# Another order of the seven products in the MLP blocks of a two-layer decoder kernel

## The chip, the cores and the metric

The kernel runs on one core of a Trainium2 chip. The metric is the device time of one execution in microseconds (us). The engines are named as in the profile: PE multiplies matrices, ACT (ScalarE) and DVE (VectorE) read the results out of PSUM and work element by element, POOL and SP mostly issue DMAs.

## The reference

Two decoder layers over 512 tokens of width 1024, then a last norm. Each layer mixes (sliding-window attention and retention, gated) and then has an MLP; the change lies mostly in the MLP.

```python
for l in range(DEPTH):
    # h = rmsnorm(x) @ w_in; attention, retention, gates; then
    x = x + mixed @ w_out
    h2 = rmsnorm(x, g_mlp)
    x = x + jnp.square(jax.nn.relu(h2 @ w_up)) @ w_down
return rmsnorm(x, g_final)
```

## The kernel before, in words

Everything is computed in f32 precision. Each operand is kept as two parts: hi, rounded on ACT (L343 for weights, L415 for intermediate values), and lo, the rest, subtracted on DVE (L344, L416). One product of f32 operands is then three matmuls (`products`, L395 to L397: hi by hi, lo by hi, hi by lo).

The weights come in units of 128 x 1024, in one list (`unit_order`). For each unit SP loads a raw tile (a pool of five), DVE may add two raw tiles (L283 in the up part, L306 in the down part), ACT and DVE split it, and PE uses it. `unit` takes the next unit of the list and splits three ahead; `split_until` loads four ahead of the split.

The MLP of a layer is worked in eight blocks of 512 hidden columns, e = 0 to 7. In block 0 the up part is a plain product; in each later block it is two *pairs* (`pair(0)`, `pair(1)`), which multiply halves with four weight units each: pairs 6 and 7 are those of block 4. The down part (`down`) of a block multiplies 2 x 2 blocks with **seven products** instead of eight (of sums and differences of the operands), each with a unit of its own and of twelve matmuls of 512 columns:

- the first into the banks a, and ACT copies a to b (L1562);
- the second into c, read out early (L1619) with sign minus;
- the third adds into b; its left operand is a sum of hidden values, split as `r<-sums` (ACT L415, DVE L416); b is read out early;
- the fourth adds into a, the fifth into c, and both are read out for good (`put`: ACT L1619 or DVE L1609);
- the sixth adds into b, which DVE reads out (L1609, into a tile eu that already holds the early part);
- the seventh adds into b again and is read out. The sixth's readout must be over, bank by bank, before the seventh's first matmul.

What was read out is sent to a DRAM tensor y by accumulating DMAs on POOL's queue (L1624). The last block of each layer takes another way at its end (layer 1's is a plain product).

At the input of a layer the first projections go into four banks at once (`group`), and meanwhile the norm is made: token sums by four small matmuls (ssq<-ones,acc, L566), their inverse root (table load and L598 on ACT, L599 on DVE), the tile wide (L601), its split sh and sl, and two matmuls ssq<-sh and ssq<-sl (L613) that spread it over all rows. `chunk(... put_q(2))` and `put_q(3)` are the two projections behind this group.

The order on each engine is made by a scheduler when the program is built; it goes by the order of the code and by its own estimate of when things are ready, and `tc.issue_after(x)` holds what is within it behind x. On the chip each engine's queue runs strictly in that order. So the code's order of products is not quite that of PE's queue: on PE, regular blocks before have 6 matmuls of the fourth, 2 of the fifth, 4 of the third, 10 of the fifth, 8 of the third, 6 of the fourth, the sixth, twelve of the next pair, the seventh.

Of the kernel before, what the change touches and what calls it, by code (L numbers as in the profile page):

```python
# [53 lines left out]
DELAY = 2  # L54
AHEAD = 4
SPLIT = 3
CLEANED = ({1: (0,)}, {})


def unit_order(layer):  # L60

    order = [("w_in", i) for i in range(4 + 2 + 8 + 2 + 4 + 2 + 2)]
    order += [("w_a", i) for i in range(4)]
    order += [("rv", part, u) for part in range(7) for u in range(2)]
    order += [("w_in", i) for i in range(24, 34)]
    order += [("w_b", i) for i in range(4)]
    order += [("w_in", i) for i in range(34, 38)]
    order += [("w_b", i) for i in range(4, 8)]
    order += [("wo", part, u) for part in range(7) for u in range(2)]
    for e in range(N_BLOCK):  # L70
        if e == 0:
            order += [("w_up", u) for u in range(4)]
        else:
            order += [("pair", 2 * e - 2 + i, part) for i in range(2) for part in range(4)]
        if layer == DEPTH - 1 and e == N_BLOCK - 1:
            order += [("w_end", k) for k in range(4)]
        else:
            order += [("block", e, part) for part in range(7)]
    return order


# [37 lines left out]
def decoder(ctx, tc, xT, x_first, w_in, w_rv, w_a, w_b, w_wo, w_up, w_pair, w_down, w_end, tables, decay, band, g_last, out):  # L119
# [182 lines left out]
    def add_block(i):  # L302
        e, part = order[i][2:]
        if part in (2, 4) and e < N_BLOCK - 1:
            raws[i] = raws.pop(i - 2)
            nc.vector.tensor_tensor(raws[i], raws[i], raws.pop(i - 1), ALU.add)  # L306

    def load_values(i):
        layer, name, part, u = order[i]
# [133 lines left out]
    def chunk(name, layer, moving, evacuate, rate=1.0, pool=ps_mm):  # L443

        hi, lo = unit(name, layer)
        n = len(moving)
        ps = bank(pool, "mm")
        pairs = [((hi[:, k * P : (k + 1) * P], lo[:, k * P : (k + 1) * P]), moving[k]) for k in range(n)]
        advance(rate)
        products(ps, pairs[: n // 2], True, False)  # L450
        advance(rate)
        products(ps, pairs[n // 2 :], False, True)
        evacuate(ps)
# [50 lines left out]
    class Forms:  # L504
# [27 lines left out]
        def part(self, j):  # L532
            return self.f[j // 2][:, 2 * (j % 2) : 2 * (j % 2) + 2, :]
# [54 lines left out]
    class Rms:  # L588
# [20 lines left out]
        def finish(self):  # L609
            self.value = tmp.tile([P, T], F32, tag="norm", name="rstd", bufs=1)  # L610
            ps = bank(ps_aux, "ssq")
            for i, part in enumerate(self.parts):
                nc.tensor.matmul(ps, ones, part, start=i == 0, stop=i == 1)  # L613
            nc.scalar.activation(self.value, ps, AF.Copy)


# [2 lines left out]
    def layer_body(layer):  # L619
# [102 lines left out]
            else {1: carried.pop(1), 2: rms_mix.prepare, 3: stats},  # L722
            {1: carried.pop(0)} if layer else None,
        )
        chunk("w_in", layer, xs, put_q(2))
        chunk("w_in", layer, xs, put_q(3), pool=ps_aux)
        turn_v()

# [668 lines left out]
        def sum_input(ks):  # L1397

            b = big("xg")
            for i in range(2):  # L1400
                g = ks + i + 4
                col = g_mlp * KD + g
                nc.scalar.activation(b[:, i, :], x[:, g, :], AF.Copy, scale=gain[:, col : col + 1])
            first = early.pop(ks)
            sums.one(ks, first)
            sums.middle(ks, first, b, (0, 1))
            sums.rest(ks, b, (2, 3))

        def block(half, tokens):
            at = slice(tokens * H, tokens * H + H)  # L1410
# [51 lines left out]
        def pair(which):  # L1462
            def multiply(ps, weights, left, moving, start=True):
                hi, lo = weights
                cols = [slice((0 if left else 4 * P) + k * P, (0 if left else 4 * P) + (k + 1) * P) for k in range(4)]
                products(ps, [((hi[:, c], lo[:, c]), m) for c, m in zip(cols, moving)], start, True, not start)

            a, e, b = (bank(ps_mm, "mm")[:, :H] for _ in range(3))
            eu, z = temp("eu"), big("z")
            part = unit("pair", layer)
            multiply(a, part, True, block(0, 0))
            nc.scalar.activation(b, a, AF.Copy)  # L1476
            multiply(e, part, False, sums[0])
            nc.scalar.activation(eu[:, :H], e, AF.Copy)
            part = unit("pair", layer)
            multiply(b, part, True, sums[1], False)  # L1480
            nc.scalar.activation(eu[:, H:], b, AF.Copy)
            multiply(a, part, False, block(1, 0), False)
            nc.scalar.activation(z[:, 0, :H], a, AF.Relu)
            if which:
                second(z, slice(0, 1), SOON)
            part = unit("pair", layer)
            multiply(b, part, True, sums[2], False)
            nc.vector.scalar_tensor_tensor(z[:, 1, H:], b, -1.0, eu[:, :H], ALU.mult, ALU.subtract)
            multiply(e, part, False, block(1, 1), False)
            nc.vector.tensor_tensor(z[:, 0, H:], e, eu[:, H:], ALU.add)  # L1490
            nc.scalar.activation(z[:, :, H:], z[:, :, H:], AF.Relu)
            if which:
                second_late(z)
            part = unit("pair", layer)
            multiply(b, part, True, sums[3], False)
            nc.scalar.activation(z[:, 1, :H], b, AF.Relu, scale=-1.0)
            if which:
                second(z, slice(1, 2), SOON)
                second_rest(z)
            elif plain:  # L1500
                first_plain(z)
            else:
                first_two(z)
# [34 lines left out]
        def down(e, into, meanwhile=None):  # L1538
            def multiply(ps, moving, start=True):
                hi, lo = unit("block", layer)  # L1540
                for m in range(2):
                    at = slice(m * P, (m + 1) * P)
                    pairs = []
                    for k, (uh, ul) in enumerate(moving):
                        cols = slice(k * T, (k + 1) * T)
                        pairs.append(((uh[:, at], ul[:, at]), (hi[:, cols], lo[:, cols])))
                    products(ps[m], pairs, start, True, not start)

            b11 = [(first_hi[:, k, :], first_lo[:, k, :]) for k in range(2)]
            b21, b22 = (  # L1550
                [(u_two[:, k, at], u_two[:, 2 + k, at]) for k in range(2)] for at in (slice(0, H), slice(H, T))
            )
            if e == N_BLOCK - 1:
                sums.free()
            a, c = ([bank(ps_mm, "mm") for _ in range(2)] for _ in range(2))
            b = [bank(ps_aux, "b") for _ in range(2)]
            multiply(a, b11)
            with tc.issue_after(latest[0]):
                for m in CLEANED[last].get(e, ()):
                    nc.tensor.matmul(b[m], ones, xh[:, 0, :], start=True, stop=True)  # L1560
            for m in range(2):
                nc.scalar.activation(b[m], a[m], AF.Copy)  # L1562
            multiply(c, u_forms[0])
            for m in range(2):
                into.early(1, 1, m, c[m], -1)
            multiply(b, u_forms[1], False)
            for m in range(2):
                into.early(0, 1, m, b[m], 1)
            if meanwhile:
                with tc.issue_after(last_second[0]), tc.issue_after(last_second[1]):  # L1570
                    meanwhile()
            multiply(a, b21, False)
            for m in range(2):
                into.put(0, 0, m, a[m], 1)
            if e == N_BLOCK - 1:
                state["hold"] = state["next"] + 3
            multiply(c, b22, False)
            for m in range(2):
                into.put(0, 1, m, c[m], 1)
            multiply(b, u_forms[2], False)  # L1580
            for m in range(2):
                into.put(1, 1, m, b[m], -1)
            into.last_but_one()
            multiply(b, u_forms[3], False)
            if e == N_BLOCK - 1:
                into.first_weights()
            for m in range(2):
                into.put(1, 0, m, b[m], -1)
            into.end()
# [146 lines left out]
        def first_hooks():  # L1736
            used = []

            def at0():
                used.append(column_factors())  # L1740
                sum_input(0)

            def at1():
                if last:
                    used.append(bank(ps_aux, "xt"))
                    for n in range(NB):
                        turn_x(used[n % 2], n, 1)

            return at0, at1
# [196 lines left out]
```

## Time and profile before

| | us |
|---|---|
| median of three runs | 1447.37 (1445.71 to 1448.91) |
| the profiled execution | 1446.45 |
| its span (first to last instruction) | 1444.4 |
| PE busy | 1431.3 |
| DVE busy | 1166.0 |
| ACT busy | 969.6 |
| POOL busy | 222.0 |

The granted clock was 0.999 in the mean. Busy times overlap, and a matmul's end is modelled, so small stalls of PE count as busy; a stall shows in the starts of two matmuls: in a run without waits, matmuls of 512 columns start 0.23 us apart and those of 256 columns 0.11 us. In the lists of waits a row says who waited for whom, the total, how many times and the longest; in timelines a row has start, duration, engine, line, operation, the tiles written and read, and in brackets the idle time ahead of it with what ended it.

### The profile page before, as it was taken

The numbers are of one execution on the slowest core, as the hardware profiler recorded it, in microseconds if no ns is written. First come the engines' busy times: TensorE is split into PE (matmuls) and PEld (weight loads), VectorE is DVE, ScalarE is ACT, GpSimd is POOL, SyncE is SP. The second block draws the span as 40 slices with busy tenths as digits, with TensorE's granted clock in tenths as the row PEclk, the third lists the DMA queues.
The fourth block names the chain that finished last, engine by engine and source line by source line (L and its number), as shares of the span: only waits on it lengthen the run. The fifth ranks groups of instructions, "written<-read, shape, count | busy, mean of one in ns | idle before, by whom it ended". The sixth has DMA issues, their size and how long they took to land.

```text
span 1444.4 us, 22150 instructions
## 1 busy us (share of the span) xinstructions
PE 1431.3 (99%) x8041; PEld 1246.5 (86%) x8041; DVE 1166.0 (81%) x1762; ACT 969.6 (67%) x1592; POOL 222.0 (15%) x329
## 2 busy tenths in 40 slices
PE   9999999999999999999999999999999999999998
PEld 7888888888988999998888888888889799999987
DVE  6978876966998888888878789677779978888885
ACT  7657555553687777777756575565437878777775
POOL 0011012112101111112201110112120011111120
PEclk9999999999999999999999999999999999999999
DMA  7598359899745777676955983797875477777664
GB/s 267 179 288 225 103 162 305 238 245 253 234 130 197 192 201 194 176 185 182 314 172 177 290 224 105 214 299 219 227 204 185 144 203 198 195 199 195 179 188 153
DMA packets 96429, 297.57 MB, mean 206 GB/s; under 512 B 11329, under 2 KB 11457, under 8 KB 90433
## 3 DMA queue, kind: packets, MB, share of 16 engines
q0 software_dynamic: 35936, 125.58, 37.6%
q1 hardware_dynamic: 59664, 169.27, 33.6%
q8 instruction: 63, 1.03, 0.3%
q10 hardware_dynamic: 720, 1.31, 0.2%
q14 instruction: 46, 0.37, 0.1%
HBM read 256.54 MB, written 115.87 MB: 258 GB/s over the span
## 4 chain that ended last, share of the span: by engine, by line
PE 97%; ACT 2%; DVE 1%; DMA 0%; issue 0%; ACTq 0%; DVEq 0%
PE mm L395 23%; PE mm L396 23%; PE mm L397 23%; PE wo L1301 5%; PE b L395 3%; PE b L396 3%; PE b L397 3%; PE rv L395 2%; PE rv L397 2%; PE rv L396 2%; PE mm L410 2%; PE score L778 1%; PE pT L743 1%; PE r L396 1%; PE r L397 1%; PE r L395 1%
## 5 line engine op out<-in xcount | busy, mean ns | idle before, releaser
L343 ACT ACTIVATE hi<-raw 128x1024 fp32r<-128x1024 f32 (+1 forms) x387 | 394.4, 1022 | 247.9 <-PE mm L396 131.3
L344 DVE TENSOR_TENSOR lo<-raw,hi 128x1024 fp32r<-128x1024 f32 (+1 forms) x388 | 452.3, 1173 | 96.3 <-ACT hi L343 94.8
L395 PE MATMUL mm<-xh,hi 128*128 128x512 f32 (+1 forms) x976 | 340.9, 353 | 2.3 <-ACT xh L418 1.1
L396 PE MATMUL mm<-xl,hi 128*128 128x512 f32 (+1 forms) x976 | 341.2, 352 | 0.0
L397 PE MATMUL mm<-xh,lo 128*128 128x512 f32 (+1 forms) x976 | 338.0, 352 | 0.0
L395 PEld LDWEIGHTS mm<-xh,hi 128*128 128x128 f32 x976 | 183.2, 188 | 28.4 <-ACT xh L418 1.8
L396 PEld LDWEIGHTS mm<-xl,hi 128*128 128x128 f32 x976 | 183.4, 188 | 24.0
L397 PEld LDWEIGHTS mm<-xh,lo 128*128 128x128 f32 x976 | 182.3, 188 | 23.6
L397 PE MATMUL mm<-r,lo 128*128 128x256 f32 (+1 forms) x608 | 186.2, 306 | 0.0
L396 PE MATMUL mm<-r,hi 128*128 128x256 f32 (+1 forms) x608 | 186.1, 306 | 0.0
L395 PE MATMUL mm<-r,hi 128*128 128x256 f32 (+1 forms) x608 | 184.0, 307 | 0.5 <-ACT mm L1476 0.5
L395 PEld LDWEIGHTS mm<-r,hi 128*128 128x128 f32 x608 | 114.1, 188 | 8.5 <-ACT mm L1476 0.7
L396 PEld LDWEIGHTS mm<-r,hi 128*128 128x128 f32 x608 | 114.2, 188 | 7.8
L397 PEld LDWEIGHTS mm<-r,lo 128*128 128x128 f32 x608 | 114.1, 188 | 6.3
L1624 POOL DMA_DIRECT2D y<-eu x56 | 62.2, 1347 | 365.4 <-DVE eu L1609 364.8
L396 PE MATMUL mm<-lo,r 128*128 128x512 f32 (+1 forms) x276 | 104.9, 389 | 0.0
L397 PE MATMUL mm<-hi,r 128*128 128x512 f32 (+1 forms) x276 | 101.3, 387 | 0.0
L395 PE MATMUL mm<-hi,r 128*128 128x512 f32 (+1 forms) x276 | 98.4, 390 | 1.0 <-ACT eu L1619 0.6
L395 PE MATMUL b<-hi,r 128*128 128x512 f32 x180 | 70.5, 392 | 1.6 <-DVE eu L1609 1.2
L396 PE MATMUL b<-lo,r 128*128 128x512 f32 x180 | 70.2, 390 | 0.0
L283 DVE TENSOR_TENSOR raw<-raw 128x512 f32<-128x512 f32 x56 | 38.5, 687 | 36.6 <-DMA raw<-w_pair_in 27.8
L397 PE MATMUL b<-hi,r 128*128 128x512 f32 x180 | 67.8, 390 | 0.0
(323 smaller groups left out, 2705.6 us busy)
## 6 DMA issues: line engine op xcount, KB each, us to landing
raw<-w_in_in SPq DMA_DIRECT2D x73, 512.0 KB, 6.3
sums_down<-w_down_in POOLq DMA_DIRECT2D x30, 1024.0 KB, 11.2
sums_up<-w_pair_in POOLq DMA_DIRECT2D x56, 512.0 KB, 10.7
raw<-w_down_in SPq DMA_DIRECT2D x45, 512.0 KB, 7.7
raw<-w_pair_in SPq DMA_DIRECT2D x84, 256.0 KB, 3.7
y<-y POOLq DMA_DIRECT2D x63, 256.0 KB, 9.6
y<-eu POOLq DMA_DIRECT2D x61, 256.0 KB, 8.2
raw<-sums_down SPq DMA_DIRECT2D x30, 512.0 KB, 7.9
```

The costliest lines, as they stand in the source:

```text
L283: nc.vector.tensor_tensor(raws[i][:, at], last[:, LEFT], last[:, RIGHT], ALU.add)
L343: state["high"] = nc.scalar.activation(hi[:, at], raw[:, at], AF.Copy).ins
L344: nc.vector.tensor_tensor(lo[:, at], raw[:, at], f32(hi[:, at]), ALU.subtract)
L395: nc.tensor.matmul(ps, ah, bh, start=start and i == 0, stop=False, **more)
L396: nc.tensor.matmul(ps, ah, bl, start=False, stop=False, **more)
L397: latest[0] = nc.tensor.matmul(ps, al, bh, start=False, stop=stop and i == n - 1, **more).ins
L410: latest[0] = nc.tensor.matmul(ps, w[:, cols(j, c)], moving[k][low], start=first, stop=bool(final)).ins
L743: nc.tensor.transpose(pt[:, i * P : (i + 1) * P], sm[:, at : at + P], ident)
L778: nc.tensor.matmul(ps[:, g * w : (g + 1) * w], q_s[g][:, c, at], part[:, keys], start=i == 0, stop=i == 1)
L1301: latest[0] = nc.tensor.matmul(o, w[:, cols], v, start=start and first and n % 2 == 0 and w is hi and v is vh, stop=final and w is lo, ski ...
L1624: nc.gpsimd.dma_start(y[:, 2 * j + m, i * T : (i + 1) * T], t, **how)
```

## The change

It has four parts. The units of the blocks 0 to 6 are listed with the sixth product ahead of the fifth, `down` issues them in that order, and the raw sums (now L308) are written into the newer of the two tiles. A pair(0) is held behind the latest matmul, the seventh product's. In block 0 the last of the input sums is issued behind the sixth and fifth product instead of ahead of the fourth. And the projection put_q(2) is held behind the norm's products.

```diff
--- before.py
+++ after.py
@@ -54,6 +54,7 @@
+BLOCK_ORDER = (0, 1, 2, 3, 5, 4, 6)
@@ -75,7 +76,7 @@
-            order += [("block", e, part) for part in range(7)]
+            order += [("block", e, part) for part in (BLOCK_ORDER if e < N_BLOCK - 1 else range(7))]
@@ -302,8 +303,9 @@
         if part in (2, 4) and e < N_BLOCK - 1:
-            raws[i] = raws.pop(i - 2)
-            nc.vector.tensor_tensor(raws[i], raws[i], raws.pop(i - 1), ALU.add)
+            other = raws.pop(i - (2 if part == 2 else 3))
+            raws[i] = raws.pop(i - (1 if part == 2 else 2))
+            nc.vector.tensor_tensor(raws[i], raws[i], other, ALU.add)
@@ -610,7 +612,7 @@
-                nc.tensor.matmul(ps, ones, part, start=i == 0, stop=i == 1)
+                self.summed = nc.tensor.matmul(ps, ones, part, start=i == 0, stop=i == 1).ins
@@ -722,7 +724,8 @@
-        chunk("w_in", layer, xs, put_q(2))
+        with tc.issue_after(rms_mix.summed):
+            chunk("w_in", layer, xs, put_q(2))
         chunk("w_in", layer, xs, put_q(3), pool=ps_aux)
@@ -1404,7 +1407,7 @@
             sums.middle(ks, first, b, (0, 1))
-            sums.rest(ks, b, (2, 3))
+            return lambda: sums.rest(ks, b, (2, 3))
@@ -1472,7 +1475,8 @@
             part = unit("pair", layer)
-            multiply(a, part, True, block(0, 0))
+            with ExitStack() if which else tc.issue_after(latest[0]):
+                multiply(a, part, True, block(0, 0))
@@ -1568,18 +1572,27 @@
                 with tc.issue_after(last_second[0]), tc.issue_after(last_second[1]):
-                    meanwhile()
+                    rest = meanwhile()
...
-            multiply(c, b22, False)
-            for m in range(2):
-                into.put(0, 1, m, c[m], 1)
-            multiply(b, u_forms[2], False)
-            for m in range(2):
-                into.put(1, 1, m, b[m], -1)
+            def fifth():
+                multiply(c, b22, False)
+                for m in range(2):
+                    into.put(0, 1, m, c[m], 1)
+            def sixth():
+                multiply(b, u_forms[2], False)
+                for m in range(2):
+                    into.put(1, 1, m, b[m], -1)
+            for part in (fifth, sixth) if e == N_BLOCK - 1 else (sixth, fifth):
+                part()
+            if meanwhile:
+                rest()
             into.last_but_one()
@@ -1738,7 +1751,7 @@
-                sum_input(0)
+                sum_input(0)()
```

The number of instructions is the same on every engine. What the scheduler makes of it is seen in the queues. In all of them the names' numbers tell the tiles apart: in block 3 of layer 0, hi_5277 is the third product's weight unit, r6_87 and r0_81 hold the split sums.

ACT, layer 0, block 3, from the split of the third product's weights (before) or the copy a to b (after) to the split of the third product's operand. First before, then after (r6_87<-sums is that operand; hi_5308 the fourth's unit, hi_5330 and hi_5329 the fifth's and the sixth's):

```order
L343 ACTIVATE hi_5277<-raw_5102 128x1024
L1562 ACTIVATE b_5304<-mm_5300 128x512
L1491 ACTIVATE z_5168<-z_5168 128x2x256
L343 ACTIVATE hi_5308<-raw_5199 128x1024
L1562 ACTIVATE b_5305<-mm_5301 128x512
L1427 ACTIVATE z_5168<-z_5168 128x2x256
L1619 ACTIVATE eu_5346<-mm_5302,columns_3811 128x512
L415 ACTIVATE r3_84<-z_5168 128x2x256
L343 ACTIVATE hi_5330<-raw_5102 128x1024
L1619 ACTIVATE eu_5348<-mm_5303,columns_3811 128x512
L415 ACTIVATE r6_87<-sums_5159 128x512
```
```order
L1566 ACTIVATE b_5304<-mm_5300 128x512
L345 ACTIVATE hi_5277<-raw_5136 128x1024
L1495 ACTIVATE z_5168<-z_5168 128x2x256
L345 ACTIVATE hi_5308<-raw_5199 128x1024
L1566 ACTIVATE b_5305<-mm_5301 128x512
L1430 ACTIVATE z_5168<-z_5168 128x2x256
L1632 ACTIVATE eu_5345<-mm_5302,columns_3811 128x512
L345 ACTIVATE hi_5329<-raw_5234 128x1024
L1632 ACTIVATE eu_5347<-mm_5303,columns_3811 128x512
L417 ACTIVATE r3_84<-z_5168 128x2x256
L1500 ACTIVATE z_5168<-mm_5166 128x256
L417 ACTIVATE r6_87<-sums_5159 128x512
```

The split of hi_5277 stood ahead of the first copy and stands behind it now; the relu of mm_5166 has come in ahead of r6_87<-sums; the sixth product's unit is split where the fifth's was.

DVE, the same block, from the split of the seventh product's unit (lo_5375) to the next pair's units. eu_5346, 5348 (after: eu_5345, 5347) are the sixth product's readouts of the banks b_5304 and b_5305, lo_5399 is the next pair's first unit, raw_5442 the sum for a unit of the pair after it:

```order
L344 TENSOR_TENSOR lo_5375<-raw_5306,hi_5374 128x1024
L1609 SCALAR_TENSOR_TENSOR eu_5368<-mm_5302,columns_3811,eu_5368 128x512
L416 TENSOR_TENSOR r0_81<-sums_5160,r0_81 128x512
L1609 SCALAR_TENSOR_TENSOR eu_5370<-mm_5303,columns_3811,eu_5370 128x512
L344 TENSOR_TENSOR lo_5399<-raw_5326,hi_5398 128x1024
L1609 SCALAR_TENSOR_TENSOR eu_5346<-b_5304,columns_3811,eu_5346 128x512
L1609 SCALAR_TENSOR_TENSOR eu_5348<-b_5305,columns_3811,eu_5348 128x512
L283 TENSOR_TENSOR raw_5442<-raw_5418 128x512
```
```order
L346 TENSOR_TENSOR lo_5375<-raw_5306,hi_5374 128x1024
L1622 SCALAR_TENSOR_TENSOR eu_5368<-mm_5302,columns_3811,eu_5368 128x512
L418 TENSOR_TENSOR r0_81<-sums_5160,r0_81 128x512
L1622 SCALAR_TENSOR_TENSOR eu_5370<-mm_5303,columns_3811,eu_5370 128x512
L346 TENSOR_TENSOR lo_5399<-raw_5326,hi_5398 128x1024
L1622 SCALAR_TENSOR_TENSOR eu_5345<-b_5304,columns_3811,eu_5345 128x512
L284 TENSOR_TENSOR raw_5442<-raw_5418 128x512
L1622 SCALAR_TENSOR_TENSOR eu_5347<-b_5305,columns_3811,eu_5347 128x512
```

The order is the same up to the first readout of b; then the sum of raw tiles (L283, after L284) has come between the readouts of the two banks.

On PE a regular block now has 6 matmuls of the fourth, 4 of the third, 2 of the fifth, 8 of the third, 4 of the fourth, 10 of the fifth, 11 of the sixth, 2 of the fourth, 1 of the sixth, the seventh, and then the pair.

ACT at the input of layer 1, where the norm is made (mm_7222 is the bank of k, whose rotation reads it twice; sh_7402 is what ssq<-sh multiplies). Before and after:

```order
L343 ACTIVATE hi_7408<-raw_7350 128x1024
L598 ACT_TABLE_LOAD
L598 ACTIVATE rcol_7397<-ssq_7392,x_75 128x4
L636 ACTIVATE rot2_7446<-mm_7222 64x512
L637 ACTIVATE rot2_7446<-mm_7222 64x512
L415 ACTIVATE sh_7402<-wide_7400 128x512
L343 ACTIVATE hi_7495<-raw_7356 128x1024
```
```order
L345 ACTIVATE hi_7408<-raw_7350 128x1024
L345 ACTIVATE hi_7495<-raw_7356 128x1024
L600 ACT_TABLE_LOAD
L600 ACTIVATE rcol_7397<-ssq_7392,x_75 128x4
L638 ACTIVATE rot2_7446<-mm_7222 64x512
L639 ACTIVATE rot2_7446<-mm_7222 64x512
L417 ACTIVATE sh_7402<-wide_7400 128x512
L616 ACTIVATE rstd_7436<-ssq_7437 128x512
```

The split of hi_7495 has moved ahead of the table load. On PE ssq<-sh stood 18 matmuls behind the token sums and stands right behind them now.

## The prediction

> **What bounds the kernel now.** I read the page first, then the waits of PE, then one regular block of the MLP on PE, ACT and DVE, row by row. The page:
>
> ```profile
> span 1444.4 us, 22150 instructions
> PE 1431.3 (99%) x8041; PEld 1246.5 (86%) x8041; DVE 1166.0 (81%) x1762; ACT 969.6 (67%) x1592; POOL 222.0 (15%) x329
> PE 97%; ACT 2%; DVE 1%; DMA 0%; issue 0%; ACTq 0%; DVEq 0%
> ```
>
> PE is the path: 97% of the chain, and outside its busy time only 1444.4 - 1431.3 = 13 us. So no reordering can win more than those, and most of them are start and tail. What PE waits for in the middle:
>
> ```profile
> PE b L395 <- DVE eu L1609: 1.2, 1, 1.2
> PE mm L395 <- DVE rot L640: 0.6, 1, 0.6
> PE mm L395 <- ACT eu L1619: 0.6, 1, 0.6
> PE mm L395 <- ACT eu L1478: 0.5, 1, 0.5
> PE mm L395 <- ACT mm L1476: 0.5, 1, 0.5
> PE b L395 <- ACT r L415: 0.4, 1, 0.4
> PE mm L395 <- ACT r L415: 0.3, 1, 0.3
> ```
>
> These seven single waits are 4.1 us. None repeats in every block, so the regular blocks run without a stall, and all that the change can take away is about 4 us. DVE (81%) and ACT (67%) are busy beside PE, in fixed queues. Whether they still keep ahead when their queues are rearranged decides the time: a stall that every block has counts twelve times (blocks 1 to 6 of both layers).
>
> **The change, part by part.** No instruction is added or removed on any engine. What moves is which work stands behind which. I lay block 3 of layer 0 out anew, with the durations that it has now. ACT in it, from the copy that opens the third product's banks:
>
> ```profile
> 543.05 0.58 ACT L1562 ACTIVATE b<-mm 128x512 f32<-128x512 f32 x1 [0.44 <-PE mm L397]
> ...
> 544.07 1.05 ACT L343 ACTIVATE hi<-raw 128x1024 fp32r<-128x1024 f32 x1
> ...
> 548.66 0.64 ACT L415 ACTIVATE r<-sums 128x512 fp32r<-128x512 f32 x1
> 549.18 1.06 ACT L343 ACTIVATE hi<-raw 128x1024 fp32r<-128x1024 f32 x1
> 550.13 0.38 ACT L1496 ACTIVATE z<-mm 128x256 f32<-128x256 f32 x1
> 550.39 0.64 ACT L415 ACTIVATE r<-sums 128x512 fp32r<-128x512 f32 x1
> ```
>
> And PE where the third product begins (the row of two is the start of the fifth product: two starts in 0.45 us, 0.23 each) and where its first bank ends (553.55):
>
> ```profile
> 549.25 0.61 PE L395 MATMUL mm<-hi,r 128*128 128x512 f32 x2
> 549.70 0.39 PE L395 MATMUL b<-hi,r 128*128 128x512 f32 x1
> ...
> 553.55 0.62 PE L397 MATMUL b<-hi,r 128*128 128x512 f32 x2
> ```
>
> *First wait: the third product.* It needs the split r<-sums at 548.66, which ends at 549.30; PE comes at 549.70. Now ACT waits at 543.05 for PE's first product, and that cannot move. Today the third product's weights (hi) are split ahead of this copy, in ACT's idle time. In the new order that split stands behind the copy, and so does the relu L1496, which today follows r<-sums. Both now lie between 543.05 and the split: 550.13 - 549.18 = 0.95 for a split and 550.39 - 550.13 = 0.26. So r<-sums ends at 549.30 + 1.21 = 550.51 and PE is released at 550.55, with 0.04 for the way (an estimate; from ACT's 553.08 + 1.07 = 554.15 to DVE's start at 554.17 it is 0.02 in the rows further below). PE comes two rows earlier than today, at 549.25, as the fifth product's two rows now stand behind. Stall 1.30 us. Lower end: 549.30 + 0.04 - 549.25 = 0.1, if ACT found the 1.21 us elsewhere; but behind 543.05 no row above has idle time ahead of it.
>
> *Second wait: the fifth product's two rows.* They need its hi split, which stands behind r<-sums and one more r<-sums. From the new start 549.87: two splits of 549.18 - 548.66 = 0.52 each, then 1.06 for hi: 551.97, PE released at 552.00. PE has done four rows of the third product from 550.55 and stands there at 551.46. Stall 0.54. Between nothing and that there is only the same ACT queue, so I take it whole. The low half of the split (DVE) may cost another 0 to 0.2; I leave it at 0.
>
> *Third and fourth wait: the seventh product.* It adds into the bank of the sixth, after DVE has read it out. The cover between them is today the next pair's first twelve matmuls; now the pair stands behind the seventh, and the fifth product's rows come ahead of the sixth in PE's queue, not behind it: only two rows of the fourth product lie between. DVE today:
>
> ```profile
> 554.17 1.23 DVE L344 TENSOR_TENSOR lo<-raw,hi 128x1024 fp32r<-128x1024 f32 x1 [0.22 <-ACT hi L343]
> 555.32 0.74 DVE L1609 SCALAR_TENSOR_TENSOR eu<-mm,columns,eu 128x512 f32<-128x512 f32 x1
> 555.98 0.68 DVE L416 TENSOR_TENSOR r<-sums,r 128x512 fp32r<-128x512 f32 x1
> 556.58 0.74 DVE L1609 SCALAR_TENSOR_TENSOR eu<-mm,columns,eu 128x512 f32<-128x512 f32 x1
> 557.24 1.21 DVE L344 TENSOR_TENSOR lo<-raw,hi 128x1024 fp32r<-128x1024 f32 x1
> 558.38 1.40 DVE L1609 SCALAR_TENSOR_TENSOR eu<-b,columns,eu 128x512 f32<-128x512 f32 x2
> 560.79 0.69 DVE L283 TENSOR_TENSOR raw<-raw 128x512 f32<-128x512 f32 x1 [1.01 <-DMA raw<-sums_up]
> 561.40 2.35 DVE L344 TENSOR_TENSOR lo<-raw,hi 128x1024 fp32r<-128x1024 f32 x2
> ```
> ```profile
> 553.08 1.07 ACT L343 ACTIVATE hi<-raw 128x1024 fp32r<-128x1024 f32 x1 [1.28 <-PE mm L397]
> 554.04 0.67 ACT L1619 ACTIVATE eu<-b,columns 128x512 f32<-128x512 f32 x1
> 554.61 0.62 ACT L415 ACTIVATE r<-sums 128x512 fp32r<-128x512 f32 x1
> ```
>
> In the new order ACT reads both of the third product's banks out (two rows like 554.04) before it splits the seventh's weights (hi, today 553.08). The third product's last row starts at 552.00 + 9 x 0.23 = 554.05. ACT comes 0.49 behind a row's start (the last row of its first bank at 553.55, the read at 554.04): 554.54. With 554.61 - 554.04 = 0.57 for the read, hi runs from 555.11 to 556.18 and DVE starts lo at 556.20. Then the same DVE rows as above: 1.15, 0.66, 0.60, 0.66, 1.14; the sixth product's first bank is read from 560.41 to 561.15, PE released at 561.19. PE itself stands there 29 rows after 554.05, at 560.65. Stall 0.54. The first rank in DVE behind it is now not the second bank's read but the add L283, which waits for a load:
>
> ```profile
> 555.43 0.33 SPq L270 DMA_DIRECT2D raw<-w_pair_in  x1
> DVE raw L283 <- DMA raw<-sums_up: 8.6, 9, 3.3
> ```
>
> SP issues it when lo of the seventh's weights ends (554.17 + 1.23 = 555.40), so it is late by as much: add at 557.43 + (560.79 - 555.40) = 562.82, read 0.61 later, ending at 564.17. PE stands at the second bank at 561.19 + 6 x 0.23 = 562.57: stall 1.64. If the data is there in time, the read ends at 561.07 + 0.61 + 0.74 = 562.42 and the stall is nothing. The wait row says 8.6 us in 9 cases, so in some of the blocks the load is not late at all; I take the middle, 0.8.
>
> Where PE has stood, the next row is slower once: 444.25 - 443.91 = 0.34 instead of 0.23 in
>
> ```profile
> 443.91 0.50 PE L395 MATMUL b<-hi,r 128*128 128x512 f32 x1 [1.20 <-DVE eu L1609]
> 444.25 0.40 PE L396 MATMUL b<-lo,r 128*128 128x512 f32 x1
> ```
>
> Two of the four waits are followed by work that PE sets (the third product's rest, the next pair): 0.2. A regular block: 1.30 + 0.54 + 0.54 + 0.8 + 0.2 = 3.4 us; twelve of them **+40.6**. Ends: 1.30 alone (+16) and with the late load in all (4.2 us, +51). The pair behind the seventh product costs no more itself: its copy (L1476) has the pair's next twelve matmuls as cover, as it has now in block 0.
>
> *The norm at the second layer's input.* Ordering the q chunk behind the norm's products puts the first of them (ssq<-sh) directly behind the token sums, without the 18 matmuls between.
>
> ```profile
> L566 PE MATMUL ssq<-ones,acc x8: 164/250/250, 743.5 to 744.2; 128*128 128x1 f32 x8
> 740.94 1.28 ACT L598 ACT_TABLE_LOAD   x1
> 744.45 0.26 ACT L598 ACTIVATE rcol<-ssq,x 128x4 f32<-128x4 f32 x1 [2.23 <-PE ssq L566]
> 746.78 0.63 ACT L415 ACTIVATE sh<-wide 128x512 fp32r<-128x512 f32 x1
> 744.96 0.69 DVE L601 TENSOR_TENSOR wide<-ident,rcol 128x512 f32<-128x512 f32 x1
> ```
>
> The table load lies today ahead of the sums, hidden. In the new queue a further hi split stands ahead of it, of a buffer that PE frees with the group's last matmul, 0.2 ahead of the sums: 743.3 + 0.49 + 0.95 + 1.28 puts rcol at 746.0 instead of 744.45. From rcol's start wide takes 745.65 - 744.45 = 1.2, two rotary copies on ACT meanwhile about as long, then sh 0.63: 747.9, and PE has stood since 744.4. I take **+3.7** (with the load out of the way it is 2.2).
>
> *Sums of the input, first blocks and gains.* In both block 0s DVE's last input sum moves behind the fifth product, the 1.2 us wait above goes, others of the kinds above come; bound 0 to one regular block each, I take +1 each, **+2**. Of the 4.1 us of waits above I count **-3.5** (the one at rstd's tables and those of the last pair go, part of layer 1's block 0 stays).
>
> Sum: 40.6 + 3.7 + 2 - 3.5 = +42.8. The profiled execution took 1446.45 us (span 1444.4 and 2.05 around it): 1489.3; the median of the three runs is 0.9 above it: **1490**.
>
> **The clock.** The page's clock row stands at nine in all forty slices, and after 1.2 us of idle time the second matmul is at 0.23 again:
>
> ```profile
> PEclk9999999999999999999999999999999999999999
> ```
>
> [...]
>
> **Rivals.**
> 1. *Only the first wait is real* (the rest of the block catches up, as DVE or ACT have more slack than one block's rows show): 12 x 1.4 + 3.7 - 3.5 = +17, 1464. For it: three of four waits are worked from sums of ten rows. Against: those rows are without idle time.
> 2. *Not slower.* ACT's queue has the slack after all, above all if the third product's hi split finds its place before the copy; then only the 4.1 us go: 1443. It decides at r<-sums: it must end by 549.2, 1.3 us ahead of my 550.51. Against it: the copy's wait for PE at 543.05 is one in each block, and the rows behind it are back to back.
> 3. *The load is late in all blocks*, and later than today as PE's stalls shift it: +51 and more, 1500 to 1508.
> [...]
>
> **How the numbers follow.** My forecast, blocks with 2.6 to 4.3 us each, 1478 to 1502: 0.74. Rival 1: 0.10; rival 2: 0.05, of which faster 0.03; rival 3: 0.07; rival 4: 0.04. The range 1472 to 1504 holds the forecast, the nearer part of rival 1 and half of rival 3. A difference of 0.2% (2.9 us) is about what a measurement can tell: faster 0.03, same 0.02, slower 0.95.
>
> **What would show it.** In the new profile PE's busy share falls to 96%. PE's waits should list b <- ACT r<-sums about twelve times at 1.3 us, mm <- ACT hi about twelve times at 0.5, and b <- DVE eu up to 24 times, the second bank's in an irregular size; ssq <- ACT sh once at 3.7. The seven waits quoted should be mostly gone. I am wrong if r<-sums ends before PE reaches the third product, or if DVE reads the sixth product's banks out with time left.

## The result, and the profile after

The changed kernel took 1495.54 us in the median of four runs (1494.82 to 1497.37), the kernel before 1447.82 in four: slower by 47.7 us, a ratio of 1.033 with a 95% interval of 1.032 to 1.035. The forecast was 1490 with a range of 1472 to 1504.

The page of the changed kernel, first PE's share, then the chain of work that ended last, then the clock row:

```profile
span 1495.2 us, 22116 instructions
PE 1448.4 (97%) x8041; PEld 1244.5 (83%) x8041; DVE 1170.3 (78%) x1762; ACT 968.8 (65%) x1592; POOL 226.7 (15%) x329
PE 80%; ACT 10%; DMA 4%; DVE 3%; issue 2%; SPq 0%; DVEq 0%; ACTq 0%
PEclk9999999999999999999999999999999999999999
```

PE's share of the chain falls from 97% to 80%. ACT does no more work than before (968.8 us against 969.6), but is now 10% of the chain: the same work has come to stand in PE's way. (The counts of the engines are those of before; the total in the first row, 22116 against 22150, holds waiting instructions too.) Here is what PE waits for (us in total, times, longest):

```profile
PE b L397 <- DVE eu L1622: 13.3, 24, 1.3
PE b L397 <- ACT r L417: 12.7, 11, 1.2
PE mm L397 <- ACT hi L345: 4.2, 12, 1.3
PE ssq L615 <- ACT sh L417: 3.9, 1, 3.9
PE mm L412 <- ACT xh L420: 1.3, 1, 1.3
```

The first three rows stand almost wholly for the twelve regular blocks, the fourth is the norm. Of the 24 waits of the first row, twelve are for the sixth product's first bank, eleven for its second, and one is in layer 1's block 0. Block 1 of layer 0 has its first wait, the longest, under the third row (1.3 us), so that the second row has eleven. The modelled ends of matmuls make these totals a little small. From here on a *loss* is counted from start to start: the time between the starts of two neighbouring matmuls, less the 0.228 us that one of 512 columns needs. All losses together are some 32 us before and some 83 after; the difference, 50.9, is that of the two spans (50.8). The profiled execution after was the longest of its four.

Block 3 of layer 0 has all four waits:

```profile
558.09 0.50 PE L397 MATMUL b<-hi,r 128*128 128x512 f32 x1 [1.15 <-ACT r L417]
...
559.55 0.73 PE L397 MATMUL mm<-hi,r 128*128 128x512 f32 x2 [0.27 <-ACT hi L345]
...
569.06 0.47 PE L397 MATMUL b<-hi,r 128*128 128x512 f32 x1 [0.45 <-DVE eu L1622]
569.37 0.40 PE L398 MATMUL b<-lo,r 128*128 128x512 f32 x1
...
571.97 0.50 PE L397 MATMUL b<-hi,r 128*128 128x512 f32 x1 [1.29 <-DVE eu L1622]
```

The reader sees the third product, the fifth's two rows, the seventh's first bank and its second bank, each late. Behind the third of them the next start is 0.31 later, not 0.23: PE restarts slowly once. Here is ACT ahead of the first wait, and DVE around the last two:

```profile
550.58 0.58 ACT L1566 ACTIVATE b<-mm 128x512 f32<-128x512 f32 x1 [2.07 <-PE mm L399]
551.07 1.05 ACT L345 ACTIVATE hi<-raw 128x1024 fp32r<-128x1024 f32 x1
...
557.40 1.16 ACT L417 ACTIVATE r<-sums 128x512 fp32r<-128x512 f32 x2
```
```profile
568.17 0.74 DVE L1622 SCALAR_TENSOR_TENSOR eu<-b,columns,eu 128x512 f32<-128x512 f32 x1
570.56 0.69 DVE L284 TENSOR_TENSOR raw<-raw 128x512 f32<-128x512 f32 x1 [1.65 <-DMA raw<-sums_up]
571.17 0.74 DVE L1622 SCALAR_TENSOR_TENSOR eu<-b,columns,eu 128x512 f32<-128x512 f32 x1
```

ACT waits 2.07 us for PE at the copy; the third product's weights (hi at 551.07) stand behind it, and the split that PE needs ends at 557.40 + 0.64 = 558.04, that is 7.46 after the copy began. DVE has read the sixth product's first bank at 568.91, then waits 1.65 us for a load, adds, and only then reads the second bank.

The norm at the second layer's input, ACT and then PE:

```profile
764.20 1.06 ACT L345 ACTIVATE hi<-raw 128x1024 fp32r<-128x1024 f32 x1 [4.38 <-DMA raw<-w_in_in]
765.27 1.28 ACT L600 ACT_TABLE_LOAD   x1
...
768.08 0.63 ACT L417 ACTIVATE sh<-wide 128x512 fp32r<-128x512 f32 x1
```
```profile
768.76 0.80 PE L615 MATMUL ssq<-sh,ones 128*128 128x512 f32 x1 [3.86 <-ACT sh L417]
769.35 0.63 PE L397 MATMUL mm<-xh,hi 128*128 128x512 f32 x1
769.78 0.63 PE L398 MATMUL mm<-xl,hi 128*128 128x512 f32 x1
...
774.36 0.39 PE L397 MATMUL mm<-xh,hi 128*128 128x512 f32 x1
774.59 0.40 PE L398 MATMUL mm<-xl,hi 128*128 128x512 f32 x1
```

A further hi split and the table load stand ahead of the norm, as worked out. The row of the hi split names a load as what it waited for. But it starts 0.475 us after the start of the group's last matmul here and in the six other kernels with this part, and in two of those the trace names PE and the load had landed 13 us earlier: it is PE that sets the time, as the prediction had it. Behind the wait the matmuls start 0.43 us apart up to 774, and 0.23 apart from there: half speed for 5 us. The granted clock in the trace is 0.50 from 767.38 to 774.20, though the clock row of the page, with slices of 37 us, shows a nine everywhere.

### The profile page after: what moved, and what is told of

It reads as the page before. It is cut to its first block, busy times and chain, and to the rows that moved or that the text cites. A ratio compares the mean times of both kernels' runs of the same rounds, so it can differ in the third digit from the quotient of the medians.

```text
span 1495.2 us, 22116 instructions
## 1 busy us (share of the span) xinstructions
PE 1448.4 (97%) x8041; PEld 1244.5 (83%) x8041; DVE 1170.3 (78%) x1762; ACT 968.8 (65%) x1592; POOL 226.7 (15%) x329
## 3 DMA queue, kind: packets, MB, share of 16 engines
q10 hardware_dynamic: 720, 1.31, 0.2%
## 4 chain that ended last, share of the span: by engine, by line
PE 80%; ACT 10%; DMA 4%; DVE 3%; issue 2%; SPq 0%; DVEq 0%; ACTq 0%
PE mm L397 20%; PE mm L398 20%; PE mm L399 19%; PE wo L1304 5%; ACT hi L345 4%; DMA raw<-sums_up 3%; ACT r L417 2%; PE rv L399 2%; PE rv L398 2%; PE rv L397 2%; ACT eu L1632 2%; DVE lo L346 2%; PE b L399 2%; PE b L397 1%; PE b L398 1%
## 5 line engine op out<-in xcount | busy, mean ns | idle before, releaser
L1637 POOL DMA_DIRECT2D y<-eu x56 | 55.3, 1012 | 409.9 <-DVE eu L1622 409.0
L397 PE MATMUL b<-hi,r 128*128 128x512 f32 x180 | 74.3, 413 | 27.0 <-DVE eu L1622 13.3
L397 PEld LDWEIGHTS b<-hi,r 128*128 128x128 f32 x180 | 33.7, 187 | 48.2 <-ACT r L417 17.6
L399 PE MATMUL b<-hi,r 128*128 128x512 f32 x180 | 69.5, 399 | 1.3 <-DVE r L418 1.3
```

The lines of the kernel that those rows point to most:

```text
L397: nc.tensor.matmul(ps, ah, bh, start=start and i == 0, stop=False, **more)
L399: latest[0] = nc.tensor.matmul(ps, al, bh, start=False, stop=stop and i == n - 1, **more).ins
L1637: nc.gpsimd.dma_start(y[:, 2 * j + m, i * T : (i + 1) * T], t, **how)
```

## The experiments

All times are medians. A difference is taken to the kernel before as it ran on the same chip (1447.6, 1447.5 and 1446.8 us in the three groups); the changed kernel ran once, beside a kernel before of 1447.8, so that differences to it are good to about 1 us. The last input sum needed no run: built without that part, the kernel has row for row the same queue on every engine.

### The parts one by one

Each of the first three has one part of the diff above and nothing else. *Only the order* (with its sums of units):

> Only the order of the seven products is changed (with the sums of weights that go with it); the pair, the norm's products and the last input sum stay as before. Theory A, the four waits have two causes, and the order alone makes the first two: b<-ACT r<-sums 12 x 1.3 us and mm<-ACT hi 12 x 0.4 stay in the list of waits, the waits for the read-out of the sixth product (b<-DVE eu) do not appear, because the next pair's twelve matmuls still cover it: +25 to +30 us over the kernel before, 1473 to 1478. Theory B, the order alone makes all four, because the fifth product's rows no longer stand between the sixth and the seventh: b<-DVE eu is there up to 24 times too, +38 to +42, 1486 to 1490.

Measured: 1480.4, ratio 1.022 (1.021 to 1.024), +32.8. The first two rows of its waits of PE:

```profile
PE b L397 <- ACT r L417: 12.7, 11, 1.2
PE mm L397 <- ACT hi L345: 4.2, 12, 1.3
```

The first two waits are there to the tenth; the read-out waits are there in two blocks only (0.5 and 0.8 us) instead of 24 times. So theory A: the order, with the sums that go with it, makes the first and second wait and not the third and fourth. The time is 2.4 above its range.

*Only the pair* held behind the seventh product:

> Only the next pair is held back behind the seventh product. The prediction priced this part by itself at nothing: then 1446 to 1450. The other theory: the pair's twelve matmuls were the cover of the read-out of the banks into which the seventh product adds, in the old order too; then b<-DVE eu is in the list 12 times or more at 0.4 to 0.7 us each, +6 to +12, 1454 to 1460.

Measured: 1458.3, ratio 1.007 (1.005 to 1.009), +10.7. Two rows make it:

```profile
PE mm L396 <- DVE rot L641: 5.1, 1, 5.1
PE b L396 <- DVE eu L1618: 4.8, 14, 1.8
```

The read-out wait comes once in each regular block, with 0.23 to 0.28 us idle and a loss of 0.4. The prediction's price of nothing for the pair alone is wrong, and the other theory is right in kind. But half of the time is a wait of 5.1 us in the second layer's attention that neither theory had, so it is luck that the time lies in that theory's range.

*Only the norm's products* queued ahead of the q chunk:

> Only the q chunk is queued behind the norm's products. Both theories have the wait ssq<-ACT sh once at 3.9 us. Theory A, the clock falls after it as in the trace of the changed kernel (twelve matmuls at 0.43 us instead of 0.23): 3.9 + 2.8 = +6 to +7, 1453 to 1455. Theory B, the slow stretch has another cause (it belongs to the blocks ahead): then no slow stretch behind the wait, +3 to +4, 1450 to 1452.

Measured: 1459.6, ratio 1.008 (1.006 to 1.009), +12.0. The wait of 3.9 us is there, without any change in the blocks, and where the late load told of below is taken away the mean granted clock is still 0.997, against 0.999 before: theory A on the clock. The time is above both ranges, since again there is a wait of the same kind as with the pair, now pT<-DVE st of 5.6 us.

### A load that falls behind others

What DVE waits for there is the load of the rotary tables for the second layer's retention. SP's queue before, and with the norm's part alone; behind it, the wait of DVE in the latter:

```profile
815.83 0.42 SPq L630 DMA_DIRECT2D rawtab<-tables_in  x1
822.20 22.46 SPq L198 DMA_DIRECT2D raw<-w_a_in  x4
```
```profile
826.69 0.33 SPq L199 DMA_DIRECT2D raw<-w_a_in  x1
827.07 0.42 SPq L631 DMA_DIRECT2D rawtab<-tables_in  x1
```
```profile
DVE tab L632 <- DMA rawtab<-tables_in: 12.9, 1, 12.9
```

Before, the tables go out ahead of the weights w_a; with the norm's part alone one of those loads stands ahead of them in SP's queue, and waits for a split on DVE; with the pair alone there are two. The tables come late. Two kernels form the tables from a tile on the chip instead:

```diff
-            raw, t = big("rawtab"), big("tab")
-            nc.sync.dma_start(raw, tables[:, 2 * i : 2 * i + 2, :])
+            if layer and i:
+                raw, t = x[:, 0:2, :], big("tab")
+            else:
+                raw, t = big("rawtab"), big("tab")
+                nc.sync.dma_start(raw, tables[:, 2 * i : 2 * i + 2, :])
```

> The pair alone held back (as in hold_only), and the retention tables of the second layer are formed from a tile that lies on the chip, of the same size, instead of from a load: the second layer's rotations use other numbers. Theory A, 7 of the 10.7 us that the pair alone cost were this load, which stood behind two weight loads in SP's queue: the wait mm<-DVE rot of 5.1 us and the slow clock behind it (1.8) go, 1450 to 1453, and what is left is b<-DVE eu in the 12 blocks. Theory B, DVE is late there for another reason: a wait of the same size under another name, 1456 to 1460.

> The same tables without a load, with the norm's part alone (as in norm_only). Theory A: the wait pT<-DVE st of 5.6 us and the slow clock behind it go, the wait ssq<-ACT sh of 3.9 us and its slow clock stay: 1451 to 1454. Theory B: 1457 to 1461.

Measured: 1450.4, ratio 1.0024 (1.0014 to 1.0033), and 1452.9, ratio 1.004 (1.003 to 1.005). Both waits are gone, so the load was the cause. Without it the pair costs 3.6 us (12 losses of 0.4 are 4.8, a wait of 1.3 for the input of layer 1 comes too, and several old waits go) and the norm 6.1.

In the changed kernel whole, the tables again go out ahead of w_a (842.6 against 849.0), and this price is not paid. That decides the next run, *all but the norm's part*:

> The changed kernel with the norm's products queued as before. Its cost where it stands, if it is the wait of 3.9 us and 2.8 us of slow clock less the wait mm<-DVE rot of 0.6 that comes back: 6 us less than the changed kernel, 1489 to 1491. If, as with the pair alone and the norm alone, the load of the rotary tables falls behind another load in SP's queue, a wait of about 5 us in the second layer's attention comes instead and the time stays at 1494 to 1497. The price of the prediction, without the clock: 1491 to 1493.

Measured: 1501.8 (1494.9 to 1502.5), ratio 1.037 (1.034 to 1.040): 6.3 us **slower** than with the norm's part, and above all three of its forecasts. Two loads w_a stand ahead of the tables again. The profiled execution was the shortest of the four (1494.9) and shows waits of 2.1 and 1.1 us there; the other three were 7 us longer, of which no trace is at hand. Their mean granted clock was 0.997 against its 0.999: 0.002 of 1500 us, or some 6 us more at the 0.50 of the slow stretch in the trace of the changed kernel (an estimate). That PE stood longer somewhere in them, and that the tables came still later, is a guess. So parts of this kernel's change don't add up: the norm's part costs 6.1 us alone and by the medians saves 6.3 where it stands, for a reason that is only in part seen.

### Order or tile: the first wait

With the order came another thing, named in the diff but not in the prediction's working: each sum of two units is written into the newer of its two tiles. The changed kernel with that alone undone:

```diff
-            other = raws.pop(i - (2 if part == 2 else 3))
-            raws[i] = raws.pop(i - (1 if part == 2 else 2))
+            raws[i] = raws.pop(i - (2 if part == 2 else 3))
+            other = raws.pop(i - (1 if part == 2 else 2))
```

> The changed kernel whole, but each sum of two weight units is again written into the older of its two tiles (as before), not into the newer. Queue theory (the prediction's): the third product's hi split falls behind the copy b<-a because the order of the products is another; the tile does not matter, all four waits stay, 1493 to 1498. Tile theory: the sum in the newer tile must wait until DVE has split that tile's low half for the second product, so the third product's hi split comes late; with the older tile it is ahead of the copy again, b<-ACT r<-sums falls from 12 x 1.3 to 12 x 0.3 or less and mm<-ACT hi leaves the list, 20 to 24 us less than the changed kernel, 1471 to 1476; the waits for the read-out (b<-DVE eu) stay.

Measured: 1476.4, ratio 1.019 (1.018 to 1.021), 19.1 us less than the changed kernel: the tile theory, though a little short of its 20. The list of waits has b<-ACT r once and mm<-ACT hi not at all:

```profile
PE b L397 <- DVE eu L1622: 16.4, 26, 1.6
...
PE b L397 <- ACT r L417: 0.4, 1, 0.4
```

DVE in the changed kernel, then DVE and ACT with the older tile, in the same block:

```profile
547.70 1.22 DVE L346 TENSOR_TENSOR lo<-raw,hi 128x1024 fp32r<-128x1024 f32 x1
...
549.17 1.22 DVE L308 TENSOR_TENSOR raw<-raw 128x1024 f32<-128x1024 f32 x1
```
```profile
544.63 1.22 DVE L308 TENSOR_TENSOR raw<-raw 128x1024 f32<-128x1024 f32 x1
...
546.70 1.21 DVE L346 TENSOR_TENSOR lo<-raw,hi 128x1024 fp32r<-128x1024 f32 x1
```
```profile
547.13 1.06 ACT L345 ACTIVATE hi<-raw 128x1024 fp32r<-128x1024 f32 x1 [0.58 <-PE mm L398]
548.63 0.58 ACT L1566 ACTIVATE b<-mm 128x512 f32<-128x512 f32 x1 [0.44 <-PE mm L399]
```

In the newer tile lies the second product's unit, whose lo split must have read it before the sum may overwrite it; so the sum (L308) comes behind that lo split and ends at 550.39, only 0.2 us ahead of the copy at 550.58, and in ACT's queue the hi split of the sum stands behind the copy. With the older tile the sum is done at 545.85, nearly three microseconds ahead of the copy, and hi runs in ACT's idle time.

The reverse, the kernel before with the newer tile:

```diff
-            raws[i] = raws.pop(i - 2)
-            nc.vector.tensor_tensor(raws[i], raws[i], raws.pop(i - 1), ALU.add)
+            other = raws.pop(i - 2)
+            raws[i] = raws.pop(i - 1)
+            nc.vector.tensor_tensor(raws[i], raws[i], other, ALU.add)
```

> The kernel before with one thing changed: each sum of two weight units is written into the newer of its two tiles. The products keep the order 1 to 7, pair, norm and input sums stay. Tile theory: the sum waits for the low half of the second product's split, so the third product's weights come late in the old order too; waits for r<-sums or for lo, of 0.4 to 1.3 us, appear in each of the 12 regular blocks, +10 to +20 us, 1458 to 1468. Queue theory (the order of the products makes the first wait): nothing, 1446 to 1450.

Measured: 1469.1, ratio 1.015 (1.013 to 1.017), +21.6. In the old order too the copy stands at 547.64 and the third product's hi behind it:

```profile
547.64 0.58 ACT L1563 ACTIVATE b<-mm 128x512 f32<-128x512 f32 x1 [2.08 <-PE mm L398]
548.14 1.05 ACT L344 ACTIVATE hi<-raw 128x1024 fp32r<-128x1024 f32 x1
```

So the queue theory is refuted. The wait for r<-sums is only 0.2 us idle here (a loss of 0.36 in eleven blocks, 0.90 in block 1 of layer 0), less than the tile theory said, as the third product begins two rows later in the old order. The time is just above that theory's range, and much of the +21.6 is again the tables' load (a wait of 5.6 us, and a mean granted clock of 0.996 against 0.999 before), which it did not have. And the order alone with the older tile:

> The order 1 2 3 4 6 5 7 alone, with each sum of two units in the older tile as before; pair, norm and input sums as before. Tile theory: the swap of the fifth and sixth products costs little by itself, since the pair still covers the read-out: 0.3 to 0.7 us in a block from the two rows fewer ahead of the third product, +4 to +9, 1452 to 1457. Queue theory: as with the newer tile, 1478 to 1482.

Measured: 1457.5, ratio 1.007 (1.005 to 1.009), +9.9, just above its range; against +32.8 with the newer tile. So the place of the hi split is set by the tile; the order sets how much of its lateness PE feels.

### The fourth wait

```diff
-            nc.vector.tensor_tensor(raws[i][:, at], last[:, LEFT], last[:, RIGHT], ALU.add)
+            near = ident.unsqueeze(1).broadcast_to([P, 4, P])
+            nc.vector.tensor_tensor(raws[i][:, at].rearrange("p (b q) -> p b q", q=P), near, near, ALU.add)
```

> The changed kernel, but the add that forms the next pair's weights (raw<-raw, 56 in all) reads a constant that lies on the chip, of the same size, in place of the unit that has just been loaded: the pair's products are formed with other weights in half of a unit. The same work on DVE, in the same place, without the wait for the load. Load theory (the prediction's fourth wait): of the 24 waits b<-DVE eu the longer and irregular ones, 8.7 us in eleven blocks, go, the 0.6 us ones stay: 8 to 12 us less than the changed kernel, 1484 to 1488. Rank theory (the read-out is late because an add of 0.7 us stands ahead of it, whatever it waits for): 11 waits of 0.3 to 0.4 us stay, 4 to 6 us less, 1490 to 1492.

Measured: 1486.7, ratio 1.027 (1.025 to 1.029), 8.9 us less than the changed kernel, inside the load theory's 8 to 12. The row that was 24 times 13.3 us is now:

```profile
PE b L398 <- DVE eu L1623: 3.8, 4, 1.1
```

But the 0.6 us waits of the first bank went with the fourth, which neither theory said: with no load to wait for, the scheduler put an earlier add and a read-out elsewhere in DVE's queue, and two new waits of 1.1 us came in layer 1. So it is luck that the time lies in the range, and the run is no clean measure of the load alone. That the load is what the second bank waits for is seen directly in the DVE rows at 568 to 571 above.

### The clock behind the norm

Both kernels also hold the second projection behind the group (put_q(3)) behind the norm's products in layer 1; that part of the edit is left out here.

```diff
             ps = bank(ps_aux, "ssq")
+            for _ in range(8 if self.which == 2 else 0):
+                nc.tensor.matmul(ps..., ones, ones..., start=True, stop=True)
             for i, part in enumerate(self.parts):
```

> The changed kernel with eight further 128x512 matmuls on a constant ahead of the norm's products, and all of the q chunks behind them; the products of the filler are overwritten and used by nothing. The wait ssq<-ACT sh then falls from 3.9 us to 3.86 - 8 x 0.23 = 2.0 us. Theory A, PE's clock falls because of the length of the idle time: no slow stretch, the matmuls behind ssq<-sh come every 0.23 us. Theory B, it falls because of what lies around it (eight matmuls of one column, the drain before the norm), whatever the idle time: twelve matmuls at 0.43 us again.

> The same with three further matmuls: the wait is 3.86 - 3 x 0.23 = 3.2 us. [...] Theory B: the slow stretch as before.

One execution each, so the traces tell and not the times (1495.7 and 1498.2). PE with eight, then with three further matmuls:

```profile
767.11 0.49 PE L617 MATMUL ssq<-sh,ones 128*128 128x512 f32 x1 [1.89 <-ACT sh L417]
...
768.87 0.42 PE L397 MATMUL mm<-xh,hi 128*128 128x512 f32 x1
769.10 0.61 PE L398 MATMUL mm<-xl,hi 128*128 128x512 f32 x1
769.51 0.63 PE L399 MATMUL mm<-xh,lo 128*128 128x512 f32 x1
...
772.50 0.41 PE L397 MATMUL mm<-xh,hi 128*128 128x512 f32 x1
772.75 0.39 PE L398 MATMUL mm<-xl,hi 128*128 128x512 f32 x1
```
```profile
769.36 0.80 PE L617 MATMUL ssq<-sh,ones 128*128 128x512 f32 x1 [3.04 <-ACT sh L417]
...
770.68 0.63 PE L397 MATMUL mm<-xh,hi 128*128 128x512 f32 x1
771.11 0.63 PE L398 MATMUL mm<-xl,hi 128*128 128x512 f32 x1
```

Neither theory holds as it was put. After only 1.9 us of idle time (and 0.23 more) PE begins at full rate, and is slow later: its starts are 0.41 to 0.43 us apart from 769.10 to 772.50. After 3.0 us it is slow at once (0.43 from 770.68 to 771.11), up to 774.1. Yet after 2.1 us, in the kernel without the norm's part, the mean granted clock is 0.999, as in the kernel before, against 0.997 in both kernels here. So the length of the idle time alone does not give this. The granted clock that the traces record shows more. It is 1.00 from 4.56 to 1441.57 us in the kernel before; in the changed kernel it is 1.00 from 9.62, 0.50 from 767.38, 1.00 from 774.20 and 0.50 from 1491.00. From one change to the next these are 421 and 222, 2 and 210 times 3.413 us.

What goes with the falls in these two traces is how much PE does within one such stretch. Divide each trace into windows of 3.413 us at these changes, and count a matmul of 512 columns as 0.228 us from its start and smaller ones in proportion, so that 15 fill a window. Then the clock fell behind three full-clock windows, with no matmul's work (before, from 1438.16; after, from 763.96) and with 4.9 (after, from 1487.59), and behind no others; the emptiest of the others has 6.3 (after, from 514.79). Two of the three lie at a kernel's end. With eight further matmuls the 3.41 us ahead of the first slow start, at 769.10, hold six. So few falls show no exact limit.

## Why the prediction was right, and where it was off

The regular blocks, loss by loss, in the terms of the sum:

| term | predicted for one | measured loss | in all regular blocks |
|---|---|---|---|
| first wait | 1.30 | 1.31 (1.42 in block 1 of layer 0) | 15.9 |
| second wait | 0.54 | 0.44 (0.26 in that block) | 5.1 |
| third wait | 0.54 | 0.61 (0.70 in that block) | 7.4 |
| fourth wait | 0.8, 0 to 1.64 | 0.35 to 1.45, mean 0.79 in 11 blocks | 8.7 |
| restart | 0.2 | 0.11 behind each wait | about 5 |

37.1 for the waits and about 5 for restarts, 42 against 40.6. The first wait came out as the queue said: r<-sums ends 7.46 us after the copy's start both in the working (543.05 to 550.51) and in the trace. That rests on the new queue, which was read off correctly; what put hi behind the copy was the tile, not the order of products as the rivals and the text supposed, and a reader who wanted to mend the change by its order would have mended the wrong line.

The third and fourth wait: right in size (the fourth by a middle taken between 0 and 1.64), half right in cause. The pair was said to cost no more itself, since its own cover is unchanged. It does: it *was* the cover of the read-out, and without it the first bank's wait is there in the old order too. The fourth needs both parts. With the older tile the three parts cost 9.9 + 3.6 + 6.1 = 19.6 one by one (the pair's and the norm's without the late tables), and 28.8 together; the 9.2 between are about the size of the second bank's waits in that kernel (9.3 us), which neither part alone has. That is a match of sizes; that the waits need both parts is seen in the lists.

What was too small, and makes the 5.5 us by which 1490 fell short:

- The norm: the wait was 3.86 idle (4.1 from start to start), predicted 3.7, though the terms given for it add up to 3.5 (747.9 less 744.4). But the sum held no slow clock; in the trace twelve matmuls were 0.2 later each, 2.5 us.
- The first blocks and gains, predicted -1.5 together: 4.8 us of new waits in the two block 0s, and 5.3 of the old losses gone, some -0.5. The prediction put its +2 down to the last input sum and the waits around it; that part of the diff changes no queue, and 3.7 of the 4.8 are there with the order alone.
- Not foreseen: mm<-ACT xh at the turn into layer 1, a loss of 1.45, when the group's first projection waits for the layer's input. It is there with the pair alone, too.
- The start: the full clock was granted at 9.62 us after and at 4.56 before, and the thirteenth matmul behind the eight warm<-ones starts at 10.26 and 8.81, 1.5 us later. With the order alone and the older tile the starts were 0.43 apart up to 12.6, though nothing at the start differs: it says nothing of the change.

Against that the profiled execution was the longest of its four, so that the losses (50.9) are above the medians' difference (47.7). Two smaller readings were off: PE's busy share fell to 97%, not 96%, and the 13 us outside PE's busy time are no bound on what a reordering could win, as the losses before are some 32 us from start to start.

Of the rivals: only the first wait (1464) and no slowdown fell with the list of waits. The late load was partly there, as the forecast had it. A fall of PE's clock in the blocks (rival 4, put at 0.04) did not happen: with four idle times of up to 1.3 us in some 15 us, the granted clock is 1.00 all the way from 9.62 to 767.38 and from 774.20 to 1491.00. All seven old waits went, but three of them stood in the block 0s, where the new ones came.

## What to carry to other kernels

When operands are added or split in place, ask which tile the result goes into: the tile decides which reader must be done first, and so where the whole chain behind it falls in its engine's queue; here that choice cost 19 us and the reorder that came with it about half as much. Before moving filler work, name what it covers now, not only what covers it. And don't add up the prices of parts that were measured one at a time: each part also reshuffles the load queue, and a late load that costs 6 to 7 us (5.9 and 7.1 here) can appear with one part and go with the next.

## What was not expected of the hardware

- PE's half rate did not go by the length of an idle time alone: 1.9 us brought it once, six matmuls later, and with 2.1 us in another kernel the mean granted clock stayed 0.999. In the traces before and after, the granted clock changed on a grid of 3.413 us, and fell behind three windows with at most 4.9 of 15 matmuls' work and behind none with 6.3 or more. In the starts of the matmuls a slow stretch lasted 3.4 us (eight further matmuls) to 5.0 us (the changed kernel), which costs 0.2 us for each matmul of 512 columns in it (0.43 against 0.23).
- The full clock at the kernel's start was granted at 4.56 us before and at 9.62 after. In the kernel with the order alone and the older tile, with the same queue there, the first fourteen matmuls behind the eight warm<-ones took 6.14 us (6.47 to 12.61), and 3.34 before (5.92 to 9.26): 2.8 us more, nearly as much as the 3.6 of a part that was to be told apart.
- The tables' load of 512 KB took 16.2 us from issue to landing with the norm's part alone and 13.6 before: most of its lateness is the later issue, not a slower load.
